# A hybrid decoder block on one core: the middle of the kernel, from the second half's memory values to the first group of the up projection, moves from the scheduler to a written list of steps

## The chip, the cores and the metric

One core of a Trainium2 chip runs the whole kernel. The metric is the device time of one execution in microseconds (us). The core has TensorE (PE in the profile, PEld for its weight loads), VectorE (DVE), ScalarE (ACT), GpSimd (POOL) and SyncE (SP), each with an in-order queue of its own. SP issues most DMAs; the ones that accumulate (destination += source) are issued by POOL, as software DMAs.

## The reference

One decoder block on x (1024 tokens of 1024 channels) in float32, cut to what matters here:

```python
x = x + concat(norm(fox_attention(h)), norm(stick_breaking(h))) @ w_out   # h = rmsnorm(x)
h, m = rmsnorm(x), rmsnorm(mem)                                            # 256 memory rows
q, k, v = h @ w_mq, (m @ w_mkv).split(2)                                   # 4 heads of 256
x = x + softmax(q @ k.T / 16) @ v @ w_mo                                   # memory attention
u = causal_dwconv(rmsnorm(x) @ w_up)                                       # 1024 -> 2 x 2816, width 3
x = x + (silu(gate) * val) @ w_down
return rmsnorm(x)
```

## The kernel before

Every float32 product is made of three matmuls on rounded parts: an operand is rounded (`hi`, ACT or POOL) and the remainder taken on DVE (`lo`), then `mm3` multiplies hi hi, hi lo and lo hi into one PSUM bank of 128 x 512. PSUM is used as eight banks under the tags P (3), S (3) and T (2).

The token rows are worked on as two halves of 512 (`th` 0 and 1), the attention before them by pairs of heads. Up to the first half of the output projection the order of every engine's instructions is written out ahead by a planner (`Plan`, with a cost and a due time `at` for each step) and issued inside `tc.manual_schedule`. From there on the scheduler of the language orders the work, by priorities of its own and by what is ready.

The stretch of this change comes after that. `mem_probs(th)` makes the queries, scores and softmax of the memory attention for one half; `mem_values` turns the probabilities (tile `pm`), splits them and multiplies by the values (`pom`). The output projection of the memory attention and the up and down projections save one product in eight, by Strassen's scheme in Winograd's form: halves of the operands are added and subtracted, seven smaller products are made, and the results are combined. For the memory projection:

- the first half's output, negated, lies split in `om0h` and `om0l`; the second's goes to `s1`, `a22` and, as copies to be summed onto, `s3` and `a22n12` (tiles `om1q`, `om1k`, `mos`);
- `onto_a` issues a DMA on POOL that accumulates: s1 += a22, s3 and a22n12 += both parts of om0 and so on, each on 512 KB (`[128, 1024]` float32), or 256 KB for rows of `xr`;
- two products with om0 (`pmo`) run by themselves: s = 0 goes to `u` (ACT) and from there, and from the bank, into the rows `xr`; s = 1 into `xr`;
- the weights `w_mo` are loaded once more in quarters (`mow`: `b11`, `b12`, `b22`, `b21`), and combined on DVE and POOL;
- `mo_product` makes the five others in the order p5, p7, p6, p3, p4, each of four steps f with two splits (`moa`, `mob`) and four banks; `done5` to `done4` add their banks to `xr` and `u`.

Then `ffn_norm(0)` norms rows 0 to 3 (square on ACT, mean on DVE, power on POOL, scale on DVE), turns them (`ptn`) and keeps them plain (`f1`) and split (`b11`, `b21`); `ffn_norm(1)` follows for rows 4 to 7. The loop `for k in range(4)` makes the combined operands t1, t2, t3, t4 and b22 of up from them, with three POOL operations each round (L1385, L1386, L1391). Group 0's weights are prepared by `prep_gate`, `prep_sums` and `prep_a22` (sums on POOL, splits on ACT, POOL and DVE). The products p1 and p2 of groups 0 and 1 stand ahead of the transforms; then the loop over 22 groups does seven products a group, adds their banks on DVE (`cg`, `cv`), convolves and stores `a_d`.

In the attention, `fox0` adds the causal mask to a block of forget terms on POOL (tile `nm`, L631) a step ahead of use. The down projection takes every second pair of operand tiles from the pool `wk` (tag `xn`, four buffers), which also holds the normed rows and the probabilities. The descriptors of software DMAs lie in a scratch of 1024 bytes a partition.

Of the kernel before, what the change touches and what calls it, by code (L numbers as in the profile page):

```python
# [10 lines left out]
F32 = mybir.dt.float32  # L11
# [8 lines left out]
P = 128  # L20
# [32 lines left out]
class Plan:  # L53
# [3 lines left out]
    def __init__(self, bufs):  # L57
        self.bufs, self.steps, self.emitted = dict(bufs), [], 0
# [21 lines left out]
    def run(self):  # L80
# [13 lines left out]
        while len(order) < len(left):  # L94
# [3 lines left out]
            for eng, q in due.items():  # L98
                if free[eng] > now:
                    continue  # L100
                for n, (_, _, ready, s) in enumerate(q):
                    if ready > now or s.behind is not None and s.behind.begin is None:
                        continue
                    if any(self.bufs[b] < s.take.count(b) for b in s.take):
                        continue
# [11 lines left out]
                    for f in followers.get(s.seq, ()):  # L117
                        missing[f.seq] -= 1
                        if not missing[f.seq]:
                            insort(due[f.eng], (f.at, f.seq, max(p.end + p.late for p in f.after), f))  # L120
# [13 lines left out]
def hybrid_block(ctx, tc, x, mem, w, wf, pcol, bfg, fing, out):  # L134
# [155 lines left out]
    with tc.tile_pool(name="nx", bufs=4, side="right", reuse_waits="tile") as nx:  # L290
        for th in range(2):
# [8 lines left out]
            if th == 0:  # L300
                nc.scalar.dma_start(pc, pcol)
# [8 lines left out]
        for j in range(2):  # L310
# [249 lines left out]
    class Group:  # L560
# [67 lines left out]
        def fox0(self, i, c_):  # L628

            c_["nm"] = sw.tile([P, P], F32, tag="nm", name="nm", bufs=2)  # L630
            G.tensor_tensor(c_["nm"], negcs[2 * self.pr + self.a]["t"][:, i * P:(i + 1) * P], mask, op=ALU.add)  # L631
# [334 lines left out]

    x1p = ctx.enter_context(tc.tile_pool(name="x1p", bufs=1, reuse_waits="tile"))
# [3 lines left out]
    wk = mid.enter_context(tc.tile_pool(name="wk", bufs=4, reuse_waits="tile"))  # L971
# [67 lines left out]
    def mem_values(probs, evac):  # L1039
        for h in range(4):  # L1040
            pth, ptl = [], []
            for mb in range(2):
                pt = ps.tile([P, 512], F32, tag="T", name="ptm", bufs=2)
                for j in range(4):
                    T.transpose(pt[:, j * P:(j + 1) * P],
                                probs[h][:, j, mb * P:(mb + 1) * P], ident)
                if mb == 0:
                    t = sqp.tile([P, 1024], F32R, tag="sq", name="ptm0")
                    a_, b_ = t[:, :512], t[:, 512:]
                else:  # L1050
                    a_ = wrk.tile([P, 512], F32R, tag="pth1", name="pthm")
                    b_ = wrk.tile([P, 512], F32R, tag="ptl1", name="ptlm")
                split(a_, b_, pt, 1.0)
                pth.append(a_)
                ptl.append(b_)
            for cc in range(2):
                c = 2 * h + cc
                po = ps.tile([P, 512], F32, tag="P", name="pom", bufs=3)
# [23 lines left out]
    s1t, a22t = [[qkp["f"].tile([P, D], F32, tag=g, name=f"om1{g}{i}") for i in range(2)] for g in ("q", "k1")]  # L1082
# [612 lines left out]
```

## Time and profile before

| | |
|---|---|
| median of three runs (lowest, highest) | 1623.8 us (1622.86, 1624.94) |
| the profiled execution | 1618.8 us, its span 1617.0 us |
| granted TensorE clock, mean over the span | 0.986 |
| busy: PE, DVE, ACT, POOL | 1532.5, 1203.7, 788.1, 570.5 us |
| the stretch of the change | from about 830 to 1037 us of the span |

Times in the profile count from the span's start. Matmuls overlap, so their durations add up to more than the time that they take; the distance between two starts is what one costs. "[5.49 <-ACT moa L1150]" behind an instruction is how long its engine stood idle before it and what ended that. "issue" is time in which the engine waited for nothing that the profile shows.

### The profile page before, as it was taken

The page shows a single profiled execution, that of the slowest core. Times are in us where ns is not written, and L with a number is a line of the kernel's source. Part 1 is how long each engine was busy: PE and PEld are TensorE (multiplying, and loading weights), DVE is VectorE, ACT ScalarE, POOL GpSimd, SP SyncE. Part 2 cuts the span into 40 slices and gives each one's busy share as a digit, 9 for nine tenths or more (in the row PEclk, how much of TensorE's full clock was granted, in tenths as well). Part 3 has the DMA queues.
Part 4 walks back from the last instruction along what each step waited for, and adds up shares of the span by engine and source line. Part 5 has one row for each costly group of instructions (what it writes and reads, how often), then busy time and mean ns, then how long its engine had stood idle before and what let it go on. Part 6 is the DMA issues. An engine that isn't in the chain of part 4 may idle for free. (4 is left out here: it accounts for less than half of the span.)

```text
span 1617.0 us, 22066 instructions
## 1 busy us (share of the span) xinstructions
PE 1532.5 (95%) x7684; PEld 1273.8 (79%) x7684; DVE 1203.7 (74%) x2046; ACT 788.1 (49%) x1546; POOL 570.5 (35%) x663
## 2 busy tenths in 40 slices
PE   7999999999999889999998988999999999999997
PEld 7677887887888777778886766778888888788886
DVE  7377778877877873465445979999999999786566
ACT  7368768768757550134234464333333333445444
POOL 3042333432431310123135348464444453133331
PEclk9999999999999999999999999999999999999999
DMA  5211021011115546412159621222222222998782
GB/s 179 100 59 65 27 66 60 34 55 70 34 53 175 210 137 205 147 58 73 53 164 201 135 105 52 105 68 89 79 86 83 92 79 77 332 299 191 159 180 104
DMA packets 76207, 183.54 MB, mean 114 GB/s; under 512 B 8376, under 2 KB 8504, under 8 KB 75840
## 3 DMA queue, kind: packets, MB, share of 16 engines
q1 hardware_dynamic: 61392, 151.58, 27.1%
q0 software_dynamic: 14400, 30.42, 10.4%
q8 instruction: 60, 0.98, 0.2%
q14 instruction: 51, 0.42, 0.1%
q10 hardware_dynamic: 304, 0.14, 0.0%
HBM read 129.64 MB, written 33.59 MB: 101 GB/s over the span
## 5 line engine op out<-in xcount | busy, mean ns | idle before, releaser
L680 POOL TENSOR_TENSOR p<-p,aw 128x383 f32<-128x383 f32 (+4 forms) x64 | 79.8, 1248 | 176.3 <-DVE aw L674 119.4
L731 DVE TENSOR_TENSOR ptl<-pt,pth 128x512 fp32r<-128x512 f32 x192 | 103.6, 549 | 32.2 <-ACT pth L727 30.7
L727 ACT ACTIVATE pth<-pt 128x512 fp32r<-128x512 f32 x192 | 92.9, 491 | 62.9 <-PE pt L723 60.1
L208 PE MATMUL dn<-opb,opa 128*128 128x512 f32 x308 | 120.4, 391 | 2.0 <-DVE opb L1153 2.0
L209 PE MATMUL dn<-opb,opa 128*128 128x512 f32 x308 | 120.5, 391 | 0.0
L207 PE MATMUL dn<-opb,opa 128*128 128x512 f32 x308 | 118.1, 391 | 0.0
L723 PE MATMUL pt<-zid,p 128*128 128x128 f32 x576 | 96.2, 276 | 7.8 <-DVE ptl L731 7.3
L1304 POOL TENSOR_TENSOR tmp<-wv 128x512 f32<-128x512 f32 x21 | 42.1, 2003 | 163.9 <-DMA wv<-in_w_dram 152.9
L723 PEld LDWEIGHTS pt<-zid,p 128*128 128x128 f32 x576 | 72.7, 142 | 27.0 <-DVE ptl L731 9.3
L390 DVE TENSOR_TENSOR wlo<-wraw,whi 128x512 fp32r<-128x512 f32 x84 | 67.8, 834 | 21.9 <-ACT whi L385 21.3
L193 POOL TENSOR_SCALAR whi<-wraw 128x512 fp32r<-128x512 f32 x44 | 27.9, 646 | 152.0 <-PE pm L209 60.3
L740 PE MATMUL po<-ptl,v 128*128 128x512 f32 x192 | 69.5, 362 | 10.9 <-DVE ptl L731 10.5
L1408 ACT ACTIVATE yv<-cv,pc 128x1024 f32<-128x1024 f32 x22 | 27.3, 1242 | 100.0 <-DVE cv L1440 92.8
L657 POOL TENSOR_SCALAR p<-p,fx 128x128 f32<-128x128 f32 (+3 forms) x64 | 48.8, 764 | 66.8 <-DVE fx L598 53.0
L207 PE MATMUL up_p<-b,a 128*128 128x512 f32 x176 | 68.4, 392 | 4.1 <-DVE cg L1352 2.8
L385 ACT ACTIVATE whi<-wraw 128x512 fp32r<-128x512 f32 x84 | 50.3, 628 | 43.8 <-DMA wraw<-in_w_dram 19.2
L739 PE MATMUL po<-pth,v 128*128 128x512 f32 x192 | 69.8, 364 | 0.5 <-ACT pth L727 0.4
L208 PEld LDWEIGHTS dn<-opb,opa 128*128 128x128 f32 x308 | 58.3, 189 | 14.3 <-DVE opb L1153 2.4
L208 PE MATMUL up_p<-b,a 128*128 128x512 f32 x176 | 69.0, 392 | 0.0
L209 PE MATMUL up_p<-b,a 128*128 128x512 f32 x176 | 68.8, 391 | 0.0
L207 PEld LDWEIGHTS dn<-opb,opa 128*128 128x128 f32 x308 | 58.2, 189 | 12.2
L209 PEld LDWEIGHTS dn<-opb,opa 128*128 128x128 f32 x308 | 58.1, 189 | 12.2
(503 smaller groups left out, 5233.2 us busy)
## 6 DMA issues: line engine op xcount, KB each, us to landing
wraw<-in_w_dram SPq DMA_DIRECT2D x136, 256.0 KB, 2.9
a_d<-yv SPq DMA_DIRECT2D x22, 512.0 KB, 2.6
wv<-in_w_dram SPq DMA_DIRECT2D x21, 512.0 KB, 3.4
wg<-in_w_dram SPq DMA_DIRECT2D x20, 512.0 KB, 3.4
dn<-a_d POOLq DMA_DIRECT2D x32, 256.0 KB, 6.7
dn<-a_d SPq DMA_DIRECT2D x24, 256.0 KB, 9.3
dn<-in_w_dram SPq DMA_DIRECT2D x24, 256.0 KB, 7.9
xin<-in_x_dram SPq DMA_DIRECT2D x8, 512.0 KB, 4.4
```

What stands on the lines that cost most here:

```text
L207: T.matmul(o, lt[0], rt[0], start=start, stop=False)
L208: T.matmul(o, lt[0], rt[1], start=False, stop=False)
L209: T.matmul(o, lt[1], rt[0], start=False, stop=stop)
L385: A.activation(t["hi"][:, c], t["raw", n], AF.Copy)
L390: in_turn("low", lambda: V.tensor_tensor(t["lo"][:, c], t["raw", n], t["hi"][:, c].bitcast(F32), op=ALU.subtract))
L657: G.tensor_scalar(out=c_["p"], in0=c_["p"], scalar1=c_["fx"][:, 4:5], scalar2=0.0, op0=ALU.mult, op1=ALU.add)
L680: G.tensor_tensor(c_["p"][:, :n0 - 1], c_["p"][:, :n0 - 1], c_["a"][:, 1:], op=ALU.mult)
L723: T.transpose(pt[:, j * P:(j + 1) * P], self.rows[j]["p"][:, kb * P:(kb + 1) * P], ident)
L727: A.activation(t[:, 512 - n:], self.sp["pt", kb][:, 512 - n:], AF.Copy)
L731: V.tensor_tensor(t[:, 512 - n:], self.sp["pt", kb][:, 512 - n:], self.sp["th", kb][:, 512 - n:].bitcast(F32), op=ALU.subtract)
L739: T.matmul(self.po[:, c], lv, self.sp["th", kb][:, c], start=kb == 0, stop=False)
L740: T.matmul(self.po[:, c], lv, self.sp["tl", kb][:, c], start=False, stop=kb == 4 * self.g + 3)
```

## The change

The work between `mem_probs(1)` and the end of group 0's products becomes steps of a second planner, `mid_plan`, whose order is issued in one `tc.manual_schedule` for all five queues. A step may not be planned more than `AHEAD` = 12 us before its due time. On the way the work itself changes: the sums on s1, s3 and a22n12 are DVE additions from the bank; b12 - b22 is on DVE; u is accumulated into both halves of rows 0 to 3; the order of the products is p7, p5, p3, p6, p4; p5's second addition is an ACT copy and an accumulate; t1 and t2 are made from the bank by one DVE operation each, and t3 and t4 by accumulating t2 onto `f1`. Group 1's operands are prepared in the list too, and `cg` has two tiles. `wk` has seven buffers. In the attention the mask is applied by `affine_select`. The constants of the convolution are loaded after the attention, the small constants share a tile, and the scratch for descriptors is 2048 bytes. The diff, cut ("..." marks what is left out):

```diff
+                    if self.ahead is not None and now < (s.at - self.ahead) * 1e3:
+                        heappush(events, (s.at - self.ahead) * 1e3)
+                        continue
...
-    mask = const.tile([P, P], BF16, name="mask")
-    ones = const.tile([P, 1], F32, name="ones")
+    cst = const.tile([P, 8], F32, name="cst")
+    mhalf, ones, bf = cst[:, :4], cst[:, 4:5], cst[:8, 5:6]
+    V.memset(mhalf, -0.5)
     V.memset(ones, 1.0)
-    mhalf = const.tile([P, 8], F32, name="mhalf")
-    V.memset(mhalf, -0.5)
-    pc = const.tile([P, NPCOL], F32, name="pc")
-    bf = const.tile([8, 1], F32, name="bf")
+    pc = const.tile([P, C_CW], F32, name="pc")
...
-            G.tensor_tensor(c_["nm"], negcs[2 * self.pr + self.a]["t"][:, i * P:(i + 1) * P], mask, op=ALU.add)
+            G.affine_select(out=c_["nm"], in_=negcs[2 * self.pr + self.a]["t"][:, i * P:(i + 1) * P],
+                            compare_op=ALU.is_ge, fill=NEG, base=0, pattern=[[-1, P]], channel_multiplier=1)
...
+    cwp = ctx.enter_context(tc.tile_pool(name="cwp", bufs=1))
+    cw = cwp.tile([P, 192], F32, name="cw")
+    nc.scalar.dma_start(cw[:, :NPCOL - C_CW], pcol[:, C_CW:])
...
-    wk = mid.enter_context(tc.tile_pool(name="wk", bufs=4, reuse_waits="tile"))
+    wk = mid.enter_context(tc.tile_pool(name="wk", bufs=7, reuse_waits="tile"))
...
+    wmo = {i: getw(to + i) for i in range(2)}
...
+    AHEAD = 12
+    mid_plan = Plan({"P": 3, "S": 3, "T": 2, "hi": 0, "lo": 0, "raw": 3, "xn": 3, "m0": 1, "m1": 1}, AHEAD)
...
-    def evac1(c, po):
-        for t in ((s1, s3), (a22, a22n12))[c // 4]:
-            A.activation(t[c % 4], po, AF.Copy)
-    mem_values(probs, evac1)
...
-    for i in range(2):
-        onto_a(s1t[i], a22t[i])
-    for a in range(2):
-        for i in range(2):
-            onto_a(s3t[i], om_pair(a, 0, i))
-    for a in range(2):
-        for i in range(2):
-            onto_a(s4t[i], om_pair(a, 1, i))
...
+                at = 4 * h + 0.5 * mb
+                chain_ = [on(PE, 436, turn, chain_, ["T"], ["xn"] * mb, at=at, late=200)]
+                h_ = on(ACT, ROUND, high, chain_, [f"m{mb}"], at=at)
+                l_ = on(DVE, LOW, low, [h_], [], ["T"], at=at)
+                need += [h_, l_]
...
+                def plain(c=c, t=(s1, a22)[q][f]):
+                    A.activation(t, cell["po", c], AF.Copy)
+                def plus_high(c=c, t=(s3, a22n12)[q][f]):
+                    V.tensor_tensor(t, cell["po", c], om[0][c].bitcast(F32), op=add)
+                def plus_low(c=c, t=(s3, a22n12)[q][f]):
+                    V.tensor_tensor(t, t, om[1][c].bitcast(F32), op=add)
+                def onto_s1(c=c, t=s1[f]):
+                    V.tensor_tensor(t, cell["po", c], t, op=add)
+                a_ = [on(ACT, ROUND, plain, [p_], at=at)]
+                if q == 1:
+                    a_ += [on(DVE, LOW, onto_s1, [p_, made["s1", 0, f]], at=at)]
+                h_ = on(DVE, LOW, plus_high, [p_] + a_, [], ["P"], at=at)
...
+                made[("s3", "s4")[q], f] = on(DVE, LOW, plus_low, [h_], at=at + 3, lock=True)
...
-                last_u = A.activation(u[j], pm, AF.Copy, scale=-1.0).ins
-                onto_a(xr[j][:, hi_], u[j])
-            i_ = V.tensor_tensor(xr[j][:, lo_], xr[j][:, lo_], pm, op=sub)
-            if s == 1 and j == 2:
-                first_done = i_.ins
+                u_steps.append(on(ACT, ROUND, evac_u, chain_, at=at))
+                after = u_steps[-1:]
+                u_steps[-1].give.append("S")
+                accumulate(("u", j), xr[j][:, hi_], u[j], after, 45)
+            else:
+                lo_steps.append(on(DVE, LOW, evac_lo, after, [], ["S"], at=at))
+                accumulate(("ul", j), xr[j][:, lo_], u[j], lo_steps[-1:], 40)
...
+    loads = [on(DMA, 100, lambda t=t, i=i: nc.sync.dma_start(t, w[to + i]), at=8 + n / 10, late=9000 + 2300 * n)
+             for n, (t, i) in enumerate(zip(wr, (0, 1, 4, 5, 6, 7, 2, 3)))]
...
+    t1s = [on(DVE, LOW, tt(V, b11[f], b12[f], b11[f], sub), [loads[f // 2], loads[2 + f // 2]], at=24 + f, lock=True)
+           for f in range(4)]
+    t3s = [on(DVE, LOW, tt(V, b12[f], b12[f], b22[f], sub), [loads[4 + f // 2], t1s[f]], at=22 + 2.7 * f, lock=True)
+           for f in range(4)]
...
-        V.tensor_tensor(b11[f], b12[f], b11[f], op=sub)
-        G.tensor_tensor(b12[f], b12[f], b22[f], op=sub)
...
+    o7 = mo_steps(7, s3, b12, [[made["s3", f]] for f in range(4)], [[t_] for t_ in t3s], "PSTP", 31)
+    outs_at = 42.5
+    u7 = [outs(7, j, "PSTP"[j], ([], add_to(u[j], o7, j)), after=[accs["u", j], accs["ul", j]])[0] for j in range(4)]
...
+    o5 = mo_steps(5, s1, b11, [[made["s1", 1, f]] for f in range(4)], [[t_] for t_ in t1s], "STPS", 42)
+    outs_at = 53.5
+    for j in range(4):
+        def copy(j=j):
+            A.activation(a22n12[j], o5[j], AF.Copy)
+        c_ = on(ACT, ROUND, copy, [split_steps[5, "out"][j]] + [accs["s4x", i] for i in range(2)], at=outs_at)
+        outs(5, j, "STPS"[j], ([j], add_to(xr[j][:, hi_], o5, j)), after=[c_])
+        finals[4 + j].append(accumulate(("p5", j), xr[4 + j][:, hi_], a22n12[j], [c_], 58))
+    for a in range(2):
+        for i in range(2):
+            accumulate(("s2", a, i), s1t[i], om_pair(a, 0, i),
+                       split_steps[5, 0][2 * i:2 * i + 2] + ([accs["s2", 0, i]] if a else []), 50 + a)
...
+    o3 = mo_steps(3, s3, b22, each([accs["s4x", i] for i in range(2)], 2), [[loads[4 + f // 2]] for f in range(4)], "PSPS", 53)
...
+    o6 = mo_steps(6, s1, b11, each([accs["s2", 1, i] for i in range(2)], 2), [[t_] for t_ in t2s], "PSPS", 64)
...
+        l_ = outs(6, j, "PSPS"[j], ([j], add_to(xr[j][:, hi_], o6, j)), ([], add_to(u[j], o6, j)), after=[u7[j]])
+        for c in (hi_, lo_):
+            finals[4 + j].append(accumulate(("v", j, c.start), xr[4 + j][:, c], u[j], l_, 76))
...
+    o4 = mo_steps(4, a22, b21, [[made["a22", 0, f]] for f in range(4)], [[t_] for t_ in t4s], "PSPS", 75)
...
+            q_ = on(ACT, 1060, square, finals[row], ["xn"], at=at + j)
+            q_ = on(DVE, 150, mean, [q_], at=at + j)
+            q_ = on(POOL, 550, power, [q_], at=at + j - 3)
+            out_.append(on(DVE, 760, scale, [q_], at=at + j))
+            spills[row] = on(DMA, 100, lambda row=row: nc.sync.dma_start(x2_d[row * P:(row + 1) * P, :], xr[row]),
+                             finals[row], at=at + j, late=3500)
...
-        A.activation(f12, p12, AF.Identity, scale=g1)
-        A.activation(f22, p22, AF.Identity, scale=g2)
-        V.tensor_tensor(f1[k], f12, f1[k], op=ALU.subtract)
-        V.tensor_tensor(w2, f22, f1[k], op=ALU.subtract)
-        V.tensor_tensor(f12, f12, f22, op=ALU.subtract)
-        A.activation(t1[k], f1[k], AF.Copy)
-        V.tensor_tensor(t1[4 + k], f1[k], t1[k].bitcast(F32), op=ALU.subtract)
-        A.activation(b22[k], f22, AF.Copy)
-        V.tensor_tensor(b22[4 + k], f22, b22[k].bitcast(F32), op=ALU.subtract)
-        A.activation(t2[k], w2, AF.Copy)
-        V.tensor_tensor(t2[4 + k], w2, t2[k].bitcast(F32), op=ALU.subtract)
-        A.activation(t3[k], f12, AF.Copy)
-        G.tensor_tensor(t3[4 + k], f12, t3[k].bitcast(F32), op=ALU.subtract)
-        G.tensor_tensor(w2, f1[4 + k], w2, op=ALU.subtract)
-        if k == 3:
-            e_ = retile(3, "t4x", F32R)
-            t4[3], t4[7] = views(e_, 2)
-        A.activation(t4[k], w2, AF.Copy)
-        G.tensor_tensor(t4[4 + k], w2, t4[k].bitcast(F32), op=ALU.subtract)
...
+        def first_t(k=k):
+            V.scalar_tensor_tensor(out=t_plain("t1", k), in0=pts[k], scalar=col(C_FFN + k), in1=f1[k],
+                                   op0=ALU.mult, op1=sub)
+        x_ = on(PE, 436, turn, norm1, ["T"], at=82 + k)
+        t_steps["t1f", k] = on(DVE, 650, first_t, [x_, f_steps[k], spills[4 + k // 2]], [], ["T"], at=88 + k)
+        t_split("t1", k, lambda k=k: t_plain("t1", k), [t_steps["t1f", k], evs[7]], 89 + k)
...
+        def second_t(k=k):
+            V.scalar_tensor_tensor(out=t_plain("t2", k), in0=pts[4 + k], scalar=ngain[:, k:k + 1], in1=t_plain("t1", k),
+                                   op0=ALU.mult, op1=add)
...
+        y_ = on(DVE, 650, second_t, [x_, t_steps["t1f", k], spills[6]], ["xn"] * (k == 2), at=92 + k)
+        h_ = on(ACT, 45 + ROUND, high, [x_] + kept, at=92 + k)
+        t_steps["b22", k] = [h_, on(DVE, 650, low, [h_, y_], [], ["T"], at=92.5 + k)]
+        t_steps["t2f", k] = y_
+        t_split("t2", k, lambda k=k: t_plain("t2", k), [y_] + split_steps[4, 1] + split_steps[3, 1], 93 + k)
+        if k % 2:
+            for q in range(2):
+                def onto_f1(q=q, i=k // 2):
+                    onto_a(tiles["f1", 2 * q + i], tiles["t2", i])
+                accs["t", q, k // 2] = on(POOL, STORE, onto_f1, [t_steps["t2f", k - 1], y_] + [f_steps[4 * q + k - 1], f_steps[4 * q + k]],
+                                          at=93 + k - 10, late=ADD)
+    for q in range(2):
+        for k in range(4):
+            t_split(("t3", "t4")[q], k, lambda q=q, k=k: f1[4 * q + k], [accs["t", q, k // 2]] + kept, 101 + 3 * q + k / 2,
+                    ["xn"] * (q == 1 and k == 2))
...
+    cgs = [None, None]
...
+            cgs[n] = retile(7, "cg1") if n else wk.tile([P, D], F32, tag="xn", name="cg0")
...
+    for k, op, q, tag, at in (("p5", "s1", "t1", "P", 96), ("p6", "s2", "t2", "S", 99), ("p3", "s4", "b22", "T", 102),
+                              ("p7", "s3", "t3", "P", 105), ("p4", "a22", "t4", "S", 108)):
+        part_steps(0, k, op, q, tag, [t_steps[q, kc] for kc in range(4)], at)
+    order = mid_plan.run()
+    with tc.manual_schedule(engines={ENG.PE, ENG.DVE, ENG.Activation, ENG.Pool, ENG.SP}):
+        for f in order:
+            f()
...
+        cg = cgs[n % 2]
+        if n > 1:
             product(n, "p1", "a11", b11, "P")
             product(n, "p2", "a12", b21, "S")
+            first_sum(n, cg)
...
-    nc = _bacc.Bacc("TRN2", target_bir_lowering=False, num_devices=1, dynamic_dma_scratch_size=1024)
+    nc = _bacc.Bacc("TRN2", target_bir_lowering=False, num_devices=1, dynamic_dma_scratch_size=2048)
```

More of the change, by code (lines that the diff above doesn't have):

```diff
@@ L119, in run @@
                         if not missing[f.seq]:
-                            insort(due[f.eng], (f.at, f.seq, max(p.end + p.late for p in f.after), f))
+                            insort(due[f.eng], (f.at, f.seq, max(p.end + p.late * (self.ahead is None or p.eng != f.eng) for p in f.after), f))
                     order.append(s)
@@ new lines, in each, with outs, add_to @@
+    def each(steps, n):
+        return [[steps[f // n]] for f in range(4)]
+    finals = {j: [] for j in range(TB)}
+    def outs(k, j, tag, *parts_, after=()):
+        last = [split_steps[k, "out"][j], *after]
+        for n, (rows, f_) in enumerate(parts_):
+            last = [on(DVE, LOW, f_, last, [], [tag] * (n == len(parts_) - 1), at=outs_at)]
+            for r_ in rows:
+                finals[r_].append(last[0])
+        return last
+    def add_to(dst, o, j, op=add, back=False):
+        return lambda: V.tensor_tensor(dst, dst if back else o[j], o[j] if back else dst, op=op)
@@ new lines, in hybrid_block, with views, retile, lazy @@
+    outs_at = 86
+    for j in range(4):
+        outs(4, j, "PSPS"[j], ([4 + j], add_to(xr[4 + j][:, lo_], o4, j)))
+        finals[j] += [accs["u", j], accs["ul", j]]
+    ti = to + 8
+    def views(t, n):
+        return [t[:, i * 512:(i + 1) * 512] for i in range(n)]
+    def retile(k, nm, dt=F32):
+        return x1p.tile([P, D], dt, tag=f"xr{k}", name=nm)
+    tiles = {}
+    def lazy(name, make):
+        if name not in tiles:
+            tiles[name] = make()
+        return tiles[name]
@@ L1265, in hybrid_block @@
[L1265 to L1293 removed]
+        V.tensor_tensor(dst[1], src, dst[0].bitcast(F32), op=sub)
@@ L1397, in hybrid_block, with first_sum @@
[L1397 to L1404 removed]
+    def first_sum(n, cg):
+        A.activation(cg[:, hi_], banks[n, "p1"], AF.Copy)
+        V.tensor_tensor(cg[:, lo_], banks[n, "p2"], cg[:, hi_], op=add)
@@ new lines, in high_low, with high @@
+    def high_low(n, o, src, after, at, eng, take=()):
+        def high():
+            if eng == ACT:
+                A.activation(op_tile(n, o)[0], src(), AF.Copy)
+            else:
+                G.tensor_scalar(out=op_tile(n, o)[0], in0=src(), scalar1=1.0, scalar2=0.0, op0=ALU.mult, op1=add)
+        h_ = on(eng, ROUND if eng == ACT else 640, high, after, take, at=at, lock=eng == POOL)
+        l_ = on(DVE, LOW, lambda: V.tensor_tensor(ops[n][o][1], src(), ops[n][o][0].bitcast(F32), op=sub), [h_],
+                at=at, lock=True)
+        op_steps[n, o] = [h_, l_]
+        return [h_, l_]
@@ new lines, in hybrid_block, with rest @@
+    norm1 = norm_steps(1, 85)
+    t_steps = {}
+    def rest(i):
+        if "rest" not in tiles:
+            t = [qkp["f"].tile([P, 1024], F32R, tag=g, name=f"bt_{g}", bufs=b) for g, b in
+                 (("q", 2), ("q", 2), ("k1", 2), ("k1", 2), ("k20", 1))]
+            t = sum([views(t_, 2) for t_ in t], [])
+            for n in range(3):
+                t += views(vp.tile([P, 2, 1024], F32R, tag="v", name=f"bt_v{n}").rearrange("p k c -> p (k c)"), 4)
+            tiles["rest"] = t
+        return tiles["rest"][i]
```

580 lines of the change are left out of this document (346 added, 234 removed).

## The prediction

> **What bounds the kernel now.** I read the page first, then busy time by stage for the stretch that the new list covers, then TensorE's waits in it, then the queues' timelines before the longest of them.
>
> ```profile
> span 1617.0 us, 22066 instructions
> PE 1532.5 (95%) x7684; PEld 1273.8 (79%) x7684; DVE 1203.7 (74%) x2046; ACT 788.1 (49%) x1546; POOL 570.5 (35%) x663
> ```
> ```profile
> 829.66:876.90 47.24, 40.42 (x201) 32.81 (x199) 20.84 (x32) 22.20 (x47) 17.90 (x19) 0.97 0.83 210
> 876.90:939.00 62.10, 59.77 (x248) 46.89 (x249) 56.06 (x84) 28.14 (x51) 29.67 (x31) 0.97 0.71 154
> 939.00:1001.50 62.50, 49.02 (x206) 36.59 (x205) 52.25 (x61) 33.26 (x57) 41.35 (x29) 0.91 0.19 68
> 1001.50:1110.00 108.50, 104.38 (x453) 85.33 (x452) 105.42 (x116) 37.83 (x48) 55.83 (x44) 0.99 0.25 86
> ```
>
> A stage row has its length, then busy time and count of PE, PEld, DVE, ACT and POOL, granted clock, DMA share, GB/s. I call the stages A to D: the second half's values and the first projection product; the five products of the memory projection; norm, transforms and first group of up; up's loop until it runs evenly. TensorE bounds the kernel, and these are stages in which it isn't kept fed.
>
> How long would they be if it were? Twelve of up's groups of 84 matmuls lie between these two stores: 19.04 us a group, 0.2267 us for a matmul of 512 columns. A 256-column one takes 0.12 us, a transpose 0.1 (eight in 0.79), by the starts in the second fence.
>
> ```profile
> 1108.38 0.33 SPq L1451 DMA_DIRECT2D a_d<-yv  x1
> ...
> 1336.84 0.33 SPq L1451 DMA_DIRECT2D a_d<-yv  x1
> ```
> ```profile
> 835.07 0.28 PE L207 MATMUL stm<-mk,qm 128*128 128x256 f32 x1
> 835.19 0.28 PE L208 MATMUL stm<-mk,qm 128*128 128x256 f32 x1
> ...
> 838.92 1.03 PE L1045 MATMUL ptm<-zid,pm 128*128 128x128 f32 x8
> 839.71 0.48 PE L207 MATMUL pmo<-whi,om0h 128*128 128x512 f32 x1
> ```
>
> Sorted by shape, A's 201 are 145 large, 24 of 256 columns and 32 transposes: 32.9 + 2.9 + 3.2 = 38.9 us, slack 8.3. B: 240 and 8, 55.2, slack 6.9. C: 150 and 56, 39.6, slack 22.9. D: 453, 102.7, slack 5.8. **In all 43.9 us. The change keeps every matmul and transpose, so no gain here can be larger.** Waits make up most of it, and matmuls at a lowered clock after them the rest (granted 0.91 in C):
>
> ```profile
> PE mo L207 <- ACT moa L1150: 5.5, 1, 5.5
> PE up_p L208 <- DVE bt_k L1381: 3.1, 1, 3.1
> PE up_p L207 <- DVE cg L1352: 2.8, 2, 1.5
> PE up_p L208 <- POOL bt_v L1385: 2.8, 1, 2.8
> PE up_p L209 <- DVE ops L1153: 2.6, 1, 2.6
> ```
>
> **The change, part by part.**
>
> *A and B: accumulates become DVE adds.* The first wait comes from POOL's queue:
>
> ```profile
> 859.93 2.12 POOL L1094 DMA_DIRECT2D xr<-mou  x2
> 866.52 0.86 POOL L1094 DMA_DIRECT2D xr<-mou  x1 [4.48 <-issue]
> 868.88 0.88 POOL L1094 DMA_DIRECT2D om1q<-om1k  x1 [1.50 <-issue]
> ```
> ```profile
> 874.68 0.63 ACT L1150 ACTIVATE moa<-om1q 128x512 fp32r<-128x512 f32 x1 [10.90 <-DMA om1q<-om1k]
> ```
>
> Between two software DMAs POOL stands 4.48 us though the profile shows nothing that it waits for. I read that as no room for more descriptors, which the larger scratch would relieve; but ten accumulates of 512 KB go from here in any case. In their place DVE gets 20 adds (8 with the high parts, 8 with the low, 4 onto s1), and ACT loses 8 copies. The four b12 - b22 go from POOL to DVE (+4 there), the first four subtractions into xr become accumulates (-4), and product p5's second add an ACT copy and an accumulate (-4). A DVE operation costs 0.60 us from start to start:
>
> ```profile
> 896.67 0.67 DVE L1172 TENSOR_TENSOR xr<-mo,xr 128x512 f32<-128x512 f32 x1
> 897.27 0.67 DVE L1171 TENSOR_TENSOR xr<-mo,xr 128x512 f32<-128x512 f32 x1
> ```
>
> In A DVE then has 8 splits, 20 adds, 4 into xr, 4 of weights, 8 b terms and 8 of the first operands: 52, or 31 us, beside 35.8 us of TensorE (144 matmuls, 32 transposes). That hides it, narrowly. A fixed list also has to follow the last scores, where the scheduler had mixed projection matmuls in between: 0 (it follows at once) to 4 us (nothing runs beside the last softmax). I take 2, since products that need no softmax head the list, and 2 for DVE: A keeps 4 of 8.3. In B each operand is prepared one ahead, and no wait at its start lowers the clock: 1.5 of 6.9.
>
> *C: transforms without POOL.* Per k, three POOL operations, seven of ACT and six of DVE become none, five and seven, with four accumulates of 512 KB in all. What POOL's additions cost DVE:
>
> ```profile
> 961.54 0.69 DVE L1376 TENSOR_TENSOR tm<-tm,f 128x512 f32<-128x512 f32 x1
> ...
> 976.55 1.75 DVE L1376 TENSOR_TENSOR tm<-tm,f 128x512 f32<-128x512 f32 x1
> ```
> ```profile
> 961.72 4.63 POOL L1385 TENSOR_TENSOR bt_v<-tm,bt_k 128x512 fp32r<-128x512 f32 x1 [6.08 <-ACT bt_k L1384]
> ...
> 976.04 1.72 POOL L1391 TENSOR_TENSOR bt_v<-tm,bt_v 128x512 fp32r<-128x512 f32 x1
> ```
>
> One and the same operation takes 0.69 us before them and 1.75 beside them; over C's 24 transforms I put the excess at 8 us. New in C are waits for accumulates and for the second norm:
>
> ```profile
> xr<-mou POOLq DMA_DIRECT2D x12, 256.0 KB, 5.3
> ...
> om1q<-om0h POOLq DMA_DIRECT2D x2, 512.0 KB, 7.4
> om1q<-om0l POOLq DMA_DIRECT2D x2, 512.0 KB, 5.9
> ```
> ```profile
> 950.28 1.04 ACT L1229 ACTIVATE xn<-xr 128x1024 f32<-128x1024 f32 x1
> ```
> ```profile
> 950.65 0.55 POOL L173 TENSOR_TENSOR rs<-rs,mhalf 128x1 f32<-128x1 f32 x1 [9.10 <-DVE rs L171]
> ```
> ```profile
> 951.23 0.75 DVE L1231 TENSOR_SCALAR xn<-xr,rs 128x1024 f32<-128x1024 f32 x1 [0.67 <-POOL rs L173]
> ```
>
> The eight accumulates into rows 4 to 7 now have one product (p4, 48 matmuls, 10.9 us) of cover where two stood: eight issues at 0.9 plus a landing of 5.3 end 2 us late. Counting from p4's end (T) without that: four squares 1.04 apart from T - 1.3, mean, power and scale, T + 4.4; t1's eight DVE operations (0.67 where one scales, 0.60 else) 5.1; the twelve of t2 and b22 7.8, with splits for up between them T + 20; issue 0.9 and landing 6.5, T + 27.5; ACT and DVE split, T + 29; the last halves of p7 and p4, T + 33. TensorE has until then p1 and p2 of two groups, five products and 32 transposes, 108 x 0.2267 + 3.2 = 27.7 us. So 5.3 idle, the 2 above, and 2 for the clock: C keeps 9 of 22.9. DVE and ACT work queued behind those splits in the fixed order waits with them.
>
> *D.* Two cg tiles in turn remove the wait for the previous group's convolution (2.8 in the rows above). By TensorE alone D would keep 2; but C and D hold 157.7 us of DVE in 171. Plus four operations (2.4), minus the 8, is 152, plus some 4 of waiting for accumulates 156: C and D together gain 15. I let D keep 4.5.
>
> *Edits at nothing.* The mask add becomes a select on POOL, 0.28 for 0.44 us, while POOL waits for DVE: 0, bounds -2 to 2.
>
> ```profile
> L631 POOL TENSOR_TENSOR nm<-negc,mask 128x128 f32<-128x128 f32 x64 | 28.1, 443 | 109.8 <-DVE fx L640 66.4 <-DMA negc<-negc_d 43.3
> ```
> ```profile
> 2.99 0.28 POOL masks.py:199 TENSOR_SCALAR_AFFINE_SELECT zid<-zid 128x128 f32<-128x128 f32 x1
> ```
>
> On SP, the weights' loads pass group 0's loads and spills join the list; all were far ahead of use, and without that cover each costs a landing, 5 us. The split constants are loaded long before use. Seven wk tiles do nothing for the down projection, whose one wait is for a load: bounds -2 to 0.
>
> ```profile
> 1406.39 0.51 PE L208 MATMUL dn<-opb,opa 128*128 128x512 f32 x1 [1.96 <-DVE opb L1153]
> ```
>
> **Sum:** slack from 43.9 to 4 + 1.5 + 9 + 4.5 = 19, a gain of 25. The profiled execution took 1618.8 us, so 1594; the median shown is 5.0 above it: **1599 us**.
>
> *A rule against it.* POOL issues an accumulate in 0.86 us here, and 28 become 30. The Trainium skill (SBUF — State Buffer, A bandwidth-pool intuition that's wrong) has a software DMA of about 620 ns take about 3100 ns beside a DVE copy, because POOL can't write its descriptors. By that page, as an estimate, the eight issues ahead of the second norm would take 25 us in place of 7, and the sum would be 1617 in place of 1599. The trace's row does not show it.
>
> **The rivals.**
>
> *DVE takes POOL's place.* For: it is busy 105.42 of 108.5 us in D, and has 5 us to spare in A. Against: the contention goes with its cause. If the 8 us stay and A loses 6 more, the gain is 11: 1613.
>
> *The accumulates land late (slower).* The fixed order holds DVE and ACT behind each. Cover: the two serial ones before p6 have 19 us, the eight before the second norm leave 3.3 for a landing, the one before t3 leaves 1.2.
>
> ```profile
> DMA to landing us min/median/max: 3.2/5.3/10.1
> ```
>
> At a landing of 15 us they cost 12.8 + 11.7 + 13.8 = 38 us; with the other 12 and some 6 for the clock 56 in place of 43.9: 1636. It decides from about 12.5. For: 10.1 occurred. Against: at a DMA share near 1, made by accumulates that go.
>
> *The list packs better.* Other products cover rows 4 to 7 and t3: slack 8, gain 36, 1588.
>
> *It does nothing.* D's backlog on DVE takes back what A to C give: 1624.
>
> **How the numbers follow.** Forecast 0.48, DVE 0.22, better 0.15, late 0.11, nothing 0.04. Faster by over 0.2% (3.2 us, about what a measurement here can tell) 0.85, within it 0.04, slower 0.11. The range reaches below the better case, 1585, and above the DVE case, 1619; late and nothing are left out, 0.15.
>
> **What would show it.** Right: no wait of 5 us before the first mo matmul; transforms on DVE near 0.7 us; up's first store 18 to 25 us earlier and 19.04 us between later ones; a wait of some 5 us before up's matmuls on t3 or t4. Wrong: DVE full from the values on while TensorE waits for its adds, accumulates landing after 10 us, or a long gap before the list's first matmul.

## The result, and the profile after

The changed kernel takes 1609.8 us (median of four runs, 1607.4 to 1612.8), the kernel before, in the same rounds, 1623.7 (1622.9 to 1624.9). The ratio is 0.9915 with a 95% interval of 0.9894 to 0.9935: a gain of 13.9 us (10.5 to 17.2) where 25 were forecast. 1609.8 lies in the range given, 11 us above the point. The profiled execution of the changed kernel took 1611.3 us (span 1609.5), that of the kernel before 1618.8, 5 below its median, so the two traces differ by 7.5 us only.

First the page's head, then busy time by stage. The windows are cut at the same events as before: last query matmul, first mo matmul, first up matmul, first and sixth store of a_d.

```profile
span 1609.5 us, 22069 instructions
PE 1533.8 (95%) x7684; PEld 1276.3 (79%) x7684; DVE 1214.5 (75%) x2066; ACT 783.7 (49%) x1530; POOL 533.9 (33%) x652
```
```profile
834.10:876.10 42.00, 40.66 (x203) 33.00 (x202) 29.73 (x48) 21.20 (x43) 10.65 (x15) 1.00 0.56 164
876.10:939.60 63.50, 58.17 (x249) 47.28 (x247) 57.37 (x81) 26.27 (x47) 31.60 (x34) 0.95 0.66 152
939.60:1007.97 68.37, 60.69 (x267) 46.86 (x265) 57.88 (x82) 37.09 (x59) 28.48 (x27) 0.95 0.42 117
1007.97:1102.65 94.68, 92.58 (x402) 75.13 (x403) 92.91 (x101) 32.36 (x42) 50.92 (x38) 1.00 0.24 84
```

Sorted by shape as in the prediction, these hold 147, 241, 211 and 402 large matmuls, 24 of 256 columns in the first, and 32, 8, 56 and 0 transposes: 39.4, 55.4, 53.4 and 91.1 us of fed TensorE. Slack is 2.6, 8.1, 15.0 and 3.6, in all 29. For before, with its windows cut at the same events (its first and sixth stores were at 1014.57 and 1108.38), it is 8.3, 6.9, 24.2 and 4.7, in all 44. The last two come from these rows:

```profile
939.50:1014.57 75.07, 61.59 (x255) 46.86 (x253) 64.78 (x75) 38.26 (x63) 46.88 (x34) 0.91 0.20 70
1014.57:1108.38 93.81, 89.69 (x393) 73.31 (x393) 90.77 (x99) 32.26 (x41) 48.28 (x37) 1.00 0.24 85
```

So A gave 5.7 us, C and D 10.3, and **B lost 1.2 where it was to give 5.4**. TensorE's waits from 830 to 1110, longest first, say with what:

```profile
PE mo L209 <- DVE mob L1270: 4.2, 1, 4.2
PE up_p L208 <- DVE cv L1754: 2.2, 2, 1.4
PE up_p L209 <- DVE b L1430: 2.2, 2, 1.6
PE up_p L208 <- ACT s L1554: 2.0, 1, 2.0
...
PE up_p L209 <- DVE bt_v L1634: 0.2, 1, 0.2
```

The 5.5 us before the first mo matmul are gone. The longest wait is new, 4.2 us for a split (`mob`). Where that split is made, the timelines of DVE and POOL show one DVE operation of 7.13 us among others of 0.68:

```profile
900.66 7.13 DVE L1270 TENSOR_TENSOR mob<-mow,mob 128x512 fp32r<-128x512 f32 x1
907.72 0.68 DVE L1303 TENSOR_TENSOR xr<-mo,xr 128x512 f32<-128x512 f32 x1
```
```profile
900.02 4.09 POOL L1246 TENSOR_TENSOR mow<-mow,mow 128x512 f32<-128x512 f32 x3
903.75 3.88 POOL L1103 DMA_DIRECT2D xr<-mos  x4
905.99 2.94 POOL L1246 TENSOR_TENSOR mow<-mow,mow 128x512 f32<-128x512 f32 x1
907.22 3.39 POOL L1570 TENSOR_TENSOR tmp<-raw_pth,raw_ptl 128x512 f32<-128x512 f32 x1
```

POOL meanwhile ran three of the subtractions for t4, issued four accumulates, and had a fourth subtraction and a sum queued.

### The profile page after: what moved, and what is told of

Read it like the earlier page. It is cut to its first block, busy times and chain, and to the rows that moved or that the text cites. A ratio compares the mean times of both kernels' runs of the same rounds, so it can differ in the third digit from the quotient of the medians.

```text
span 1609.5 us, 22069 instructions
## 1 busy us (share of the span) xinstructions
PE 1533.8 (95%) x7684; PEld 1276.3 (79%) x7684; DVE 1214.5 (75%) x2066; ACT 783.7 (49%) x1530; POOL 533.9 (33%) x652
## 4 chain that ended last, share of the span: by engine, by line
PE 54%; DVE 20%; issue 10%; DMA 6%; ACT 6%; POOL 2%; SPq 0%; POOLq 0%; DVEq 0%; ACTq 0%
PE dn L209 4%; PE dn L210 4%; PE dn L208 4%; PE pt L721 3%; DMA wraw<-in_w_dram 2%; PE pq L208 2%; PE pq L209 2%; PE up_p L208 2%; PE pq L210 2%; PE up_p L209 2%; PE up_p L210 2%; PE po L738 2%; PE pqm L210 2%; PE pqm L209 2%; PE pqm L208 2%
## 5 line engine op out<-in xcount | busy, mean ns | idle before, releaser
L1499 POOL TENSOR_TENSOR tmp<-wv 128x512 f32<-128x512 f32 x20 | 32.3, 1614 | 165.3 <-DMA wv<-in_w_dram 165.3
L738 PE MATMUL po<-ptl,v 128*128 128x512 f32 x192 | 69.6, 363 | 11.6 <-DVE ptl L729 11.3
L1729 ACT ACTIVATE yv<-cv,cw 128x1024 f32<-128x1024 f32 x22 | 27.4, 1246 | 100.2 <-DVE cv L1761 98.9
L208 PEld LDWEIGHTS dn<-opb,opa 128*128 128x128 f32 x308 | 58.1, 189 | 12.2
```

Source lines behind the costliest of these rows:

```text
L208: T.matmul(o, lt[0], rt[0], start=start, stop=False)
L738: T.matmul(self.po[:, c], lv, self.sp["tl", kb][:, c], start=False, stop=kb == 4 * self.g + 3)
```

## Experiments

Whole runs of one kernel differ by up to 11 us, so each kernel also gets a measure of its own: the time from the last query matmul to up's last matmul in its profiled execution (from start to start), called the **list time**. It is one execution's figure too. Before it is 563.5, after 551.3, 12.2 less:

```profile
829.43 0.39 PE L209 MATMUL pqm<-h_k,wlo 128*128 128x512 f32 x1
...
1392.93 0.39 PE L209 MATMUL up_p<-bt_q,s4ptl 128*128 128x512 f32 x1
```
```profile
834.12 0.40 PE L210 MATMUL pqm<-h_k,wlo 128*128 128x512 f32 x1
...
1385.44 0.40 PE L210 MATMUL up_p<-bt_q,s4ptl 128*128 128x512 f32 x1
```

| kernel | median, us | ratio to before (95%) | list time |
|---|---|---|---|
| after | 1609.8 | 0.9915 (0.9894 to 0.9935) | 551.3 |
| e2 before, edits outside the list | 1623.1 | 0.9994 (0.9981 to 1.0007) | 562.1 |
| e6 before, adds for accumulates | 1619.8 | 0.9969 (0.9955 to 0.9984) | 559.8 |
| e3 t4 on DVE | 1603.3 | 0.9871 (0.9849 to 0.9894) | 545.9 |
| e8 POOL's run ends early | 1605.2 | 0.9887 (0.9867 to 0.9906) | 548.4 |
| e7 e3 less eight adds | 1605.8 | 0.9888 (0.9870 to 0.9907) | 546.5 |
| e9 t3, t4 by POOL additions | 1617.7 | 0.9964 (0.9948 to 0.9980) | 557.3 |
| e4 after, ring of 1 KB | 1611.4 | 0.9923 (0.9907 to 0.9939) | 553.4 |
| e10 e3, ring of 1 KB | 1609.6 | 0.9925 (0.9912 to 0.9938) | 551.8 |
| e5 powers first | 1611.1 | 0.9922 (0.9906 to 0.9938) | 552.9 |
| e11 e3, and one sum on DVE | 1603.5 | 0.9882 (0.9870 to 0.9895) | 545.8 |
| e13 after, tile of 64 bytes | 1611.3 | 0.9919 (0.9899 to 0.9940) | 550.6 |
| e12 e11, tile of 64 bytes | 1604.0 | 0.9876 (0.9857 to 0.9894) | 545.2 |

**e2: the edits outside the list.** The old middle with the select, the packed constants, the late load and the ring of 2 KB.

```
-G.tensor_tensor(c_["nm"], negcs[2 * self.pr + self.a]["t"][:, i * P:(i + 1) * P], mask, op=ALU.add)
+G.affine_select(out=c_["nm"], in_=negcs[2 * self.pr + self.a]["t"][:, i * P:(i + 1) * P],
+                compare_op=ALU.is_ge, fill=NEG, base=0, pattern=[[-1, P]], channel_multiplier=1)
...
-dynamic_dma_scratch_size=1024
+dynamic_dma_scratch_size=2048
```

> The kernel before, with only the change's edits outside the list: select in place of the mask add, packed constants, the convolution's constants loaded later, DMA scratch of 2 KB. Its middle stays the old one. Theory 'head': these edits cost the 4.4 us by which the changed kernel reaches the values stage late (834.1 against 829.7 us at the last query matmul): about 1628 us here, with the last query matmul near 834. Rival 'landings': the 4.4 us are weights that landed later in that one execution (an ACT split waited 5.07 us for a load where it had waited 4.00): about 1623.7, within 2. Rival 'ring': the larger scratch alone removes POOL's 4.48 us before a software DMA and with it the 5.5 us wait of the first mo matmul: about 1618, and no gap of over 1 us put down to issue on POOL between 855 and 880.

1623.1: no change. Its last query matmul came at 836.4, late as "head" said, but without the time. e6 below, which keeps the old head, starts at 834.5, and e12, which has the new one, at 829.6. So the start varies from execution to execution (829 to 836), and the 4.7 us by which the changed kernel's profile starts its list late are not put down to the change. "Head" falls; "landings" fits, but what makes the start vary was not followed further. "Ring" was half right. POOL's gaps put down to issue are gone, but the wait of the first mo matmul stayed, as the accumulates wait for each other's landings:

```profile
867.61 2.97 POOL L1096 DMA_DIRECT2D xr<-mou  x3
...
876.31 0.86 POOL L1096 DMA_DIRECT2D mos<-om0h  x1 [1.67 <-DMA xr<-mou]
884.10 0.86 POOL L1096 DMA_DIRECT2D mos<-om0l  x1 [6.93 <-DMA mos<-om0h]
```
```profile
PE mo L205 <- ACT moa L1152: 5.1, 1, 5.1
```

**e6: part A alone**, in the kernel before.

```
-for t in ((s1, s3), (a22, a22n12))[c // 4]: A.activation(t[c % 4], po, AF.Copy)
...
+A.activation((s1, a22)[q][f], po, AF.Copy)
+V.tensor_tensor(t, po, om[0][c].bitcast(F32), op=add)
+if q == 1: V.tensor_tensor(s1[f], po, s1[f], op=add)
+V.tensor_tensor(t, t, om[1][c].bitcast(F32), op=add)
...
-for i in range(2): onto_a(s1t[i], a22t[i])
-for a in range(2):
-    for i in range(2): onto_a(s3t[i], om_pair(a, 0, i))
-for a in range(2):
-    for i in range(2): onto_a(s4t[i], om_pair(a, 1, i))
```

> The kernel before with one part of the change alone: the ten accumulates of 512 KB after the values are DVE adds straight from the products' banks (20 adds in, 8 ACT copies out); scheduler, ring and everything behind stay old. Theory 'part A': POOL's queue of accumulates made the first mo operand 5.5 us late; with the adds that wait goes, and 4 to 6 us are gained: 1618 to 1620. Rival 'DVE full': 12 us more of DVE work between the values and the first product takes it back, TensorE waits for a DVE result there: 1622 to 1626.

The ratio gives 5.0 us (2.6 to 7.3), the medians 2.5, the list time 3.7. The wait of 5.5 is gone; the longest at an mo matmul is 1.4:

```profile
PE pom L208 <- DVE ptm L217: 2.4, 1, 2.4
PE mo L208 <- DVE mob L1150: 1.5, 2, 1.4
```

Twenty adds on DVE cost less than ten accumulates in POOL's queue. But from the last query matmul to the first mo matmul it takes 46.4 us, 1.1 less than before (47.5), where the changed kernel takes 41.9: TensorE now waits 2.4 for a split ahead of the values. The five products behind it take 2.4 us less. So the adds alone take that wait away and don't give A its whole gain; the rest comes with the list, and no run separates it further.

**e3: the blocked split.** t4's subtractions move to DVE. The other queues keep their order. On DVE one other step moves, which the expectation did not foresee: the planner puts one split for p6 six operations earlier.

```
-t4s = [on(POOL, SUM, tt(G, b21[f], b21[f], b11[f], sub), [loads[6 + f // 2], t2s[f]], at=66 + f, lock=True)
+t4s = [on(DVE, LOW, tt(V, b21[f], b21[f], b11[f], sub), [loads[6 + f // 2], t2s[f]], at=66 + f, lock=True)
```

> The changed kernel with the four subtractions b21 - (b11 ...) on DVE in place of POOL; each engine's other instructions keep their order. Theory 'block': one DVE split took 7.13 us at 900.66, where its like take 0.69, while POOL ran these subtractions and four accumulates back to back; TensorE waited 4.2 us for it and then ran at a granted 0.83. Without them no DVE operation between 895 and 915 takes over 2 us, the wait is gone, up's first store comes 4 to 6 us earlier and the time is 1604 to 1606 us. Rival 'DVE full': DVE is short of time in this stretch however POOL behaves; four more operations (2.4 us) make it 1610 to 1612, with a wait of 3 us or more for a DVE result still there.

1603.3: four more operations on DVE, and 6.5 us faster than the change. "DVE full" falls and "block" holds, its bounds missed by 0.1 us (2.08 where 2 was the most) and 0.7 (the time): the split that took 7.13 us takes 0.68, the `mob` split behind it 2.08 (1.75 in the changed kernel). No wait of 4 us is left in the stretch. B is 59.1 us long for 63.7, a slack of 3.9 by the same count:

```profile
900.93 0.68 DVE L1270 TENSOR_TENSOR mob<-mow,mob 128x512 fp32r<-128x512 f32 x1
...
902.13 2.08 DVE L1270 TENSOR_TENSOR mob<-mow,mob 128x512 fp32r<-128x512 f32 x1
```
```profile
PE up_p L208 <- DVE cv L1754: 2.8, 3, 1.4
```

**e8: what holds the split.** The fourth subtraction and the sum behind the accumulates go to DVE; every other step keeps its place.

```
-t4s = [on(POOL, SUM, tt(G, b21[f], b21[f], b11[f], sub), [loads[6 + f // 2], t2s[f]], at=66 + f, lock=True)
+t4s = [on(POOL, SUM, tt(V if f == 3 else G, b21[f], b21[f], b11[f], sub), [loads[6 + f // 2], t2s[f]], at=66 + f, lock=True)
...
-x_ = total(m, r_(1, 0), r_(1, 1), add, [g_, v_] + free.get("m", []), at)
+x_ = total(m, r_(1, 0), r_(1, 1), add, [g_, v_] + free.get("m", []), at, G if n else V)
```

> The changed kernel with two of POOL's operations on DVE, the fourth subtraction for t4 and the sum behind it, so that the four accumulates behind the first three subtractions are followed by no POOL arithmetic; each engine's other instructions keep their order. Theory 'the run holds': the DVE split of 7.13 us waits for as long as POOL has two-input arithmetic at hand, through the issues between; now it ends with the third subtraction, after about 4 us, TensorE's wait falls from 4.2 to about 1 us, and the time is 1605 to 1607. Rival 'the issues hold': POOL's four issues of accumulates (3.9 us) are what keeps DVE out after the subtractions; the split still takes about 7 us and the time is 1609 to 1611.

```profile
897.68 4.08 POOL L1246 TENSOR_TENSOR mow<-mow,mow 128x512 f32<-128x512 f32 x3
901.42 3.86 POOL L1103 DMA_DIRECT2D xr<-mos  x4
```
```profile
898.33 3.99 DVE L1270 TENSOR_TENSOR mob<-mow,mob 128x512 fp32r<-128x512 f32 x1
902.25 0.68 DVE L1303 TENSOR_TENSOR xr<-mo,xr 128x512 f32<-128x512 f32 x1
```

The same split now ends 0.6 us after the third subtraction, and DVE goes on undisturbed beside the issues (1605.2, the wait 0.9). So here the issues alone held nobody, and the run of subtractions held the split to its end. As e8 gains without e3's moved split, that move isn't needed for the gain. Why the split was held on through the four issues when more arithmetic was queued behind them is not shown.

**e7: is DVE short of time there?** e3 without the eight adds of the low parts.

```
-def plus_low(c=c, t=(s3, a22n12)[q][f]):
-    V.tensor_tensor(t, t, om[1][c].bitcast(F32), op=add)
+def plus_low():
+    pass
```

> The previous variant with t4's subtractions on DVE (1603.3 us), leaving out the eight DVE adds of the low parts onto the values' sums (part of the computation is missing; all else in the same order). Theory 'DVE full': DVE sets the pace of the values and the five products, as it is busy 19.8 of 20 us there; 4.8 us less of its work gives 3 to 5 us: 1598 to 1600. Rival 'DVE deep but not last': with the blocked operation gone DVE is ahead of TensorE in this stretch, and the 4.8 us are hidden: 1603 within 1.5.

4.8 us less of DVE work brought nothing (list time 546.5 against 545.9). In A and B, DVE is busy but not the last to arrive.

**e9: C's accumulates undone.**

```
-onto_a(tiles["f1", 2 * q + i], tiles["t2", i])
+for h_ in (lo_, hi_):
+    G.tensor_tensor(tiles["f1", 2 * q + i][:, h_], tiles["f1", 2 * q + i][:, h_],
+                    tiles["t2", i][:, h_], op=add)
```

> The changed kernel with one part undone: t3 and t4 are made by eight POOL additions of 128x512 in place of the four accumulates; the list's order is kept. Theory 'contention': the additions run beside DVE's splits, whose like took 1.75 us in place of 0.69 beside POOL's additions in the kernel before; eight times about 1.05 us come back, most of it ahead of up's first group: 1614 to 1618. Rival 'landing': an accumulate's landing (8.4 us at the median here) costs as much as the additions do: 1609.8 within 2. Third: the additions are quicker than the landings and TensorE had waited for those: 1605 to 1608.

1617.7, list time 6.0 longer: the size that "contention" expected, by another way. Beside POOL's additions DVE's transforms kept their 0.74 us; they read one operand from the transposes' bank, where the old ones read two tiles. Of the splits, which read two tiles, three took longer (1.32, 1.71 and 1.11 for 0.68), others not. The longest:

```profile
967.04 10.07 POOL L1677 TENSOR_TENSOR f<-f,t2f 128x512 f32<-128x512 f32 x7 [1.89 <-DVE t2f L1657]
977.08 1.25 POOL L1570 TENSOR_TENSOR tmp<-raw_v 128x512 f32<-128x512 f32 x1
```
```profile
969.46 0.74 DVE L1657 SCALAR_TENSOR_TENSOR t2f<-ptn,ngain,t1f 128x512 f32<-128x512 f32 x1
970.12 1.71 DVE L1634 TENSOR_TENSOR t<-t2f,t 128x512 fp32r<-128x512 f32 x1
```
```profile
PE up_p L208 <- ACT s L1554: 4.0, 1, 4.0
```

What the additions cost within the list is POOL's own time: the weight sum behind them starts late, the operand s made from it is late on ACT, and TensorE waits 4.0 for it in place of 2.0. By the end of the list, at about 987, that makes 2.7 of the 6.0 us. Behind the list the scheduler of the language now takes up's first groups in another order; what of the other 3.3 comes from that and what from POOL is not separated.

**e4 and e10: the ring back at 1 KB**, in the changed kernel and in e3.

```
-dynamic_dma_scratch_size=2048
+dynamic_dma_scratch_size=1024
```

> The changed kernel with the DMA scratch back at 1 KB, all else as it is. Theory 'ring': the gaps that the profile puts down to issue, 0.4 to 4.5 us before software DMAs on POOL in the kernel before, are a ring without room; they come back around the eight accumulates at 860 to 880 and the eight at 927 to 936, and the norm's powers queued behind them come later: 1612 to 1616 us. Rival: the room isn't what held POOL (or nobody waits for these accumulates): 1609.8 within 1.5, and POOL's accumulates 0.9 us apart as now.

> The variant with t4's subtractions on DVE (1603.3 us), with the DMA scratch back at 1 KB. With 1 KB the changed kernel lost 1.6 us, but two things had moved at once there: POOL stood 0.4 to 2.4 us between accumulates and the first norm's rows came late (5.9 us of waits at the transposes in place of 1.2), while the blocked DVE split shrank from 7.13 to 4.07 us. Theory 'they cancelled': without the blocked split the ring's cost shows by itself, 4 to 6 us: 1607 to 1609, with over 4 us of waits for the normalised rows. Rival 'the ring is free': 1603 within 1.5.

In the changed kernel it seemed to cost little (1611.4, the intervals overlap): TensorE's waits for normalised rows rose from 1.2 to 5.9 us, its wait for the blocked split fell from 4.2 to 1.2. In e3 it cost 6 us (list time 551.8 against 545.9), so the two effects had largely cancelled. e10's queue on POOL, with the norm's power among the accumulates:

```profile
921.77 2.71 POOL L1103 DMA_DIRECT2D xr<-mos  x3 [2.15 <-DVE mos L1303]
927.01 0.86 POOL L1103 DMA_DIRECT2D xr<-mos  x1 [2.53 <-issue]
928.87 0.88 POOL L1103 DMA_DIRECT2D xr<-mos  x1 [1.00 <-issue]
931.29 0.86 POOL L1103 DMA_DIRECT2D xr<-mos  x1 [1.54 <-issue]
931.85 0.89 POOL L1393 TENSOR_TENSOR rs<-rs,cst 128x1 f32<-128x1 f32 x1
```
```profile
PE ptn L1409 <- DVE xn L1396: 6.0, 4, 2.5
```

**e5: the powers ahead of the eight accumulates**, which the list takes up behind the first norm's steps (pows; v_after[j] is l_).

```
-finals[4 + j].append(accumulate(("v", j, c.start), xr[4 + j][:, c], u[j], l_, 76))
...
+finals[4 + j].append(accumulate(("v", j, c.start), xr[4 + j][:, c], u[j], v_after[j] + pows, 76))
```

> The changed kernel with the eight accumulates into rows 4 to 7 after the first norm's four powers in POOL's order, not among them. Theory 'POOL queue': now the powers, 0.55 us each by themselves, stand among eight issues of 0.9 us, and the first normalised rows come 3 us late, for which TensorE waits at the first transposes and first b operands (xn 1.2, b 3.2 us). With them first, these waits fall by 2 to 3 us: 1607 to 1608. Rival 'late accumulates': the eight then land later by 4 to 5 us, the second norm (85 in the list's clock) and t1 wait for them, and it is 1610 to 1614.

1611.1: no gain. The edit moves more than POOL's order, as the planner also places transposes, norm steps and splits on the other engines anew. The waits for normalised rows fell to 0.6, but the accumulates landed later, DVE stood for one at an addition into the same rows, and the b operands behind it in its order were late:

```profile
939.75 1.89 DVE L1303 TENSOR_TENSOR xr<-mo,xr 128x512 f32<-128x512 f32 x3 [4.05 <-DMA xr<-mos]
```
```profile
PE up_p L209 <- DVE b L1436: 4.2, 1, 4.2
```

**e11: the sum behind t4 on DVE too**, on top of e3 (e8's second edit).

> The variant with t4's subtractions on DVE (1603.3 us), and the sum of POOL behind them (3.0 us at 902.37, beside which a DVE split still took 2.08 us) on DVE too. Theory: the last 1.4 us of that block go, and up's first group is ready no later: 1601 to 1603. Rival: TensorE didn't wait for that split by then; 1603 within 1.5.

1603.5, no different from e3.

**e13 and e12: the pace of up.** In the changed kernel two groups of up (168 matmuls) take 38.41 us all through the steady part of the loop, before 38.08, though TensorE waits for nothing in either. Over nine such pairs that is 3.0 us; from the sixth store to up's last matmul, with no wait left, 2.6 show:

```profile
1200.04 0.39 PE L207 MATMUL up_p<-bt_q,s4pth 128*128 128x512 f32 x1
...
1238.12 0.39 PE L207 MATMUL up_p<-bt_q,s4pth 128*128 128x512 f32 x1
```
```profile
1190.84 0.39 PE L208 MATMUL up_p<-bt_q,s4pth 128*128 128x512 f32 x1
...
1199.08 0.40 PE L208 MATMUL up_p<-t,ops 128*128 128x512 f32 x1
...
1201.89 0.40 PE L208 MATMUL up_p<-bt_k,ops 128*128 128x512 f32 x1
...
1229.25 0.39 PE L208 MATMUL up_p<-bt_q,s4pth 128*128 128x512 f32 x1
```

The twelve on t2 from 1199.08 follow each other 0.234 us apart in place of 0.2267, the next twelve 0.230, those on the odd groups' s4 0.233. By the order in which the kernel allocates its tiles, the new tile of four columns pushes t2 and the odd groups' s4 off multiples of 64 bytes (no trace shows an address). So the tile was made larger:

```
-ngain = wrk.tile([P, 4], F32, name="ngain")
+ngain = wrk.tile([P, 16], F32, name="ngain")[:, :4]
```

> The changed kernel with one tile made larger: the four columns of the negated gain take 64 bytes a partition in place of 16 (rounded up to 32), so that all tiles allocated behind them start 32 bytes further, at multiples of 64 again, as they do in the kernel before. Instructions and their order are the same. Theory 'placement': in the changed kernel the matmuls whose streamed operand (t2) or loaded operand (s4 of odd groups) lies 32 bytes off follow each other 0.234 us apart in place of 0.2267, and two groups of up take 38.41 us in place of 38.08; over 18 groups 3 us. With the larger tile two groups take 38.08 and the time is 1606 to 1607.5. Rival 'traffic': those matmuls are slowed by what other engines read at that moment; 38.41 stays, 1609.8 within 1.5.

> The same larger tile in the variant with five POOL operations on DVE (1603.5 us): by 'placement' two groups of up take 38.08 us and the time is 1600 to 1601.5; by 'traffic' 38.41 and 1603 to 1604.

```profile
1191.50 0.40 PE L208 MATMUL up_p<-bt_q,s4pth 128*128 128x512 f32 x1
...
1229.87 0.40 PE L208 MATMUL up_p<-bt_q,s4pth 128*128 128x512 f32 x1
```

38.37, and no faster (1611.3, 1604.0). With the same instructions the twelve on t2 came down to 0.230 and others rose, so where tiles lie seems to matter a little, but moving them did not bring 38.08 back. What other engines do at the moment is hardly the cause: until about 1253 the stores, which DVE ends, come 18.8 us apart while TensorE's pairs hold 38.41, so DVE slides past TensorE without the pace changing. And the pace is one figure for all runs with the same middle and tiles, whatever their waits: 38.08 in before, e2 and e6, 38.41 in the changed kernel and its eight variants with the small tile, 38.37 in e12 and e13. **These 3 us stay open.**

## Why the prediction was right or wrong

The sign and the range were right, and three of the four places: what was gained was gained in A, C and D. The gain was 11 us short by the medians, 12.8 by the list time (12.2 against 25). By stages: A gave 1.4 more than forecast, B 6.6 less, C and D 5.1 less, and the loop behind D lost 2.6.

- **A, first wait: right.** It was to keep 4 of 8.3 us and kept 2.6. e6 shows that the adds in place of the accumulates remove the wait, and that A shrinks by more than 1.1 us only with the list. e2 shows that POOL's gaps were the ring's, as read, but were not what made the operand late.
- **B: the step that failed.** "In B each operand is prepared one ahead, and no wait at its start lowers the clock: 1.5 of 6.9" left 8.1. The preparation was priced at 0.60 us an operation, with the contention of POOL and DVE looked for in C alone; t4's four subtractions stayed on POOL and came to lie in B beside the splits. e3 puts this at 5.4 us of list time, and e8, the cleaner edit, at 2.9 with a part of the block left. Without the block B keeps 3.9, still 2.4 above the forecast.
- **C and D: 5.1 us short, a reason wrong.** 13.5 were to be left and 18.6 were. The transforms run at 0.74 as forecast, but they do beside POOL too (e9): the excess of 8 us went for the most part with the new form, which reads the transposes' bank, and not with POOL's leaving (e9's three slowed splits bring back 2). What the accumulates spare in the list is POOL's time (2.7 of e9's 6.0). The 5.3 us forecast before t3 and t4 shrank to 0.2 (the row on bt_v), behind a wait of 2.0 for a weight sum: TensorE waits earlier and in more places, for normalised rows, first b operands, that sum and up's first additions. That these come near the forecast is in part luck.
- **"Edits at nothing": right** for all of them together with the ring (e2's ratio gives -1.0 us with -3.1 to 1.1); the select takes 0.30 us. **The ring had no term in the sum.** It is worth nothing to the old middle and 6 us to the list without the blocked split (e10): the list's accumulates stand ahead of the norm's powers.
- **The loop from D on** was counted at before's pace; it is 0.17 us a group slower, some 3 us, unexplained.
- **The rival "DVE takes POOL's place"** gave 1613, near the result by another way: e7 shows DVE not to be the bound in A and B; for C and D no run tests it. **"Late accumulates"** is real in small: e5 makes them late, and DVE work behind them waits as the rival said.
- **The rule against it**, a software DMA of about 3100 ns beside a DVE copy (the Trainium skill, SBUF — State Buffer, A bandwidth-pool intuition that's wrong): no run here shows it; POOL issued six of the eight in 5.36 us while DVE was busy with additions and splits. It ran no copy there, so the case that the rule speaks of was not met. What did strike is in another section of that page of the Trainium skill, Who interferes with whom: a DVE instruction with two SBUF inputs contends with a POOL instruction that reads SBUF, and one with at most one SBUF input, outside what the page calls the 2-port modes, doesn't. The traces agree (7.13 and 1.71 for two of the splits, 0.74 for the transforms). The Trainium skill's page has the winner hold for its whole instruction; here the loser stood through several.
- **What would show it:** two of five signs came: the first mo wait is gone and the transforms are at 0.74. The first store came 6.6 us earlier, not 18 to 25, or 11.3 counted from the last query matmul. The later stores are not 19.04 apart but 18.8 while DVE works off its backlog, then 19.2. The wait of 5 us before t3 or t4 is 0.2.

e3 and e11 beat both kernels: 1603.3 and 1603.5, about 20 us below before. e3 is 4 us above the forecast: more than half of the miss was one engine choice in the list, not the idea.

## What to carry to other kernels

When work goes onto a second engine, list what that engine runs at the same moment and whether both read two tiles from SBUF: one run of four POOL operations at the wrong place cost nearly a third of what the rest gained. A short, urgent instruction (a power of 0.55 us) that stands behind software DMAs in a queue comes late when the descriptor ring is too small for them (e10), so test the ring's size with the new order, not the old one. And two effects of one edit can hide each other (e4), so repeat a null result after the largest known stall is gone. When an edit goes through a planner or a scheduler, compare the order of every queue before and after: e3, e5 and e9 each moved more than was asked.

## What was not expected of the hardware

- A DVE operation of 0.68 us stood 7.13 us while POOL ran arithmetic and issues back to back, and 3.99 when POOL's run ended early. Elsewhere the two engines seem to take turns: from 985 to 989 in the changed kernel two DVE operations took 1.77 and 1.78 us beside POOL's of 1.72 and 1.74.
- With a ring of 1 KB POOL stood 0.4 to 2.5 us between 256 KB accumulates (e10); with 2 KB six were issued in 5.36 us with no gap (the changed kernel).
- The same 168 matmuls take 38.08, 38.37 or 38.41 us without a wait in the trace, one figure for each layout of the tiles; the cause is open.
- The select on POOL takes 0.30 us for 128x128 where the addition of a mask took 0.44 (means of 64 in the changed kernel and in the one before).
